# The low part of the prompt attention's values made by VectorE instead of GpSimd

## The chip, the cores and the metric

The kernel runs on one core of one Trainium2 chip. That core has five engines, each with a queue of its own that is worked in order: TensorE (PE in the profile, its weight loads PEld) multiplies matrices, VectorE (DVE) and ScalarE (ACT) work on whole tiles, GpSimd (POOL) does too and also issues some DMAs, SyncE (SP) issues the others. Tiles live in the on-chip memories, SBUF and, for TensorE's results, PSUM. The metric is the time of one execution on the device in microseconds (us), as the median of several runs; a profiled execution gives a trace beside it.

## The reference

One layer of a hybrid encoder is applied to a prompt of 2048 frames and, with the same weights, to 128 new frames (8 streams of 16) that attend to 1024 cached ones. Each layer is a normalization, one wide input projection, two branches, and an output projection:

```
h = rms_norm(x, norm_g);  z = h @ w_in
u_a, v_a, g_a, q, k, v, g_b = split(z)
y_a = u_a * spatial_gate(v_a) * silu(g_a)            # 4 groups, 128-position chunks
s = q.k / 8 - slope_h * |q_pos - k_pos|, masked by 64-position chunks, both halves c = 0, 1
a = softmax(s[0]) - lam * softmax(s[1])              # differential attention, 4 heads
o = rms_norm(a @ v) * const;  y_b = o * silu(g_b)
y = x + concat(y_a, y_b) @ w_out
```

The results are y for prompt and sample, and the new keys, values and gate rows. All of it is in 32-bit floating point.

## The kernel before

To keep precision, TensorE works on pairs: a value is split into a high part, which is the value rounded to the format fp32r, and a low part, the value less its high part. `mm3` (L491) then makes a product of three: high by high, high by low, low by high; in the profile every matmul stands under the line of a helper, L416, and every transpose under L420. `split` (L479 to L485) makes the two parts of a tile: ScalarE copies the source to the high part (L481), and then another engine subtracts (L482). That engine is VectorE unless the caller names one in the argument `lo_eng`.

The work has these stages, by the time in the profile:

- 0 to 830 us: `stream` runs the projections of the prompt and the sample (acc in the profile: 8 products of w and xT for each tile, head and kind), and beside them, woven in by `weave`, first the whole sample attention (`sample_attention`, names sk, sv, sa, sS, sO), then from 548 us on the prompt attention of the first half of the queries (`attention_a`).
- 830 to 940 us: the rest of the projections, and the output weights wo are loaded and split (tile wo, alternately by POOL and DVE).
- 940 to 1380 us: the prompt attention of the second half of the queries, beside the output products (`out_stream`, oo in the profile, with y_tp for the transposes of y and yT for their split).

The prompt attention (`attention`) goes head by head, and in a head by pairs of query tiles. `score_steps` makes the scores S in chunks of 512 keys; VectorE adds the distance term and takes the minimum (L911), ScalarE the exponential (L915), and the two halves are combined, by VectorE (L927) or by ScalarE and POOL (L930, L931). `value_steps` transposes the result (a_tp), splits it (aT) and multiplies it with the values v (oT).

The values come from `v_chunk` (L848 to L854). For each head and each 512 keys it loads vraw by a DMA on SP's queue (L851), into few buffers, and splits it into v, high and low (L853). There are 2 such chunks for each of 4 heads in the first half, and 3 and 4 for each head in the two groups of the second half: 8 + 12 + 16 = 36. The call in `v_chunk` names POOL for the subtraction. The buffers of v come free when the products oT of an earlier chunk are done; the buffer of vraw comes free when the subtraction has read it.

The order on each engine is not the order of the program's text. At the end, class `Order` takes all instructions, works out an estimated cost for each (`cost`, from its engine, kind and size), a due time, and dependences, and places them by simulating the engines (`run`); the order that it finds is fixed by added dependences. It also models that an operation of VectorE with two large inputs in SBUF and an operation of POOL shouldn't run at the same time (`port`). A changed engine of an instruction therefore changes the estimate, and with it possibly the place of every instruction after it, on every engine.

Of the kernel before, what the change touches and what calls it, by code (L numbers as in the profile page):

```python
# [55 lines left out]
def f(ap):  # L56
    return ap.bitcast(F32)
# [343 lines left out]
def trunk_step_kernel(  # L401
# [7 lines left out]
    act, dve, pool, sp = nc.scalar, nc.vector, nc.gpsimd, nc.sync  # L409
# [69 lines left out]
    def split(src, hi, lo, lo_eng=None, scale=None):  # L479
        if scale is None:  # L480
            act.copy(hi, src)  # L481
            (lo_eng or dve).tensor_tensor(out=lo, in0=src, in1=f(hi), op=ALU.subtract)  # L482
        else:
            act.activation(hi, src, AF.Copy, scale=scale)
            dve.scalar_tensor_tensor(out=lo, in0=src, scalar=scale, in1=f(hi), op0=ALU.mult, op1=ALU.subtract)  # L485
# [37 lines left out]
    def rows(ap):  # L523
        return ap.rearrange("(n p) e -> p n e", p=P)
# [323 lines left out]
    def v_chunk(sb, nv, h, g):  # L848
        r = slice(g * 512, (g + 1) * 512)
        raw = sb.tile([P, 4, P], F32, name="vraw", tag="vraw", bufs=cur["nraw"])  # L850
        sp.dma_start(raw, rows(nvp[r, h]))  # L851
        v = sb.tile([P, 2, 4, P], F32R, name="v", tag="v", bufs=nv)
        split(raw, v[:, 0], v[:, 1], pool)  # L853
        return v  # L854

    def q_load(sb, h, j, eng=sp):
# [133 lines left out]
    def attention(sb, sl, groups, wmax, nk, nv, nex, comb, eng):  # L990
# [12 lines left out]
        def v_step(key, c):  # L1003
            vs.setdefault(key, []).append(v_chunk(sl, nv, key[1], c))
            return 0
# [229 lines left out]
    with ExitStack() as left, ExitStack() as right:  # L1235
# [41 lines left out]
        for kc in range(8):  # L1277
            raw = p1.tile([P, D], F32, name="woraw", tag="x", bufs=2)
# [129 lines left out]
```

## Time and profile before

| what | us |
|---|---|
| median of 3 runs | 1381.08 (1380.9 to 1382.62) |
| profiled execution | 1381.83 |
| its span in the trace | 1380.1 |

The span is from the first to the last instruction of the trace. A busy time is the sum of an engine's instructions; "waited for" is the idle time of an engine just before an instruction and what released it. Matmuls overlap in TensorE's pipeline, and their ends are modelled, so a busy TensorE isn't yet one at its peak. The chain of waits follows the work that ended last back from the last instruction, at each step to what released it. Names such as v<-vraw say which tile is written and which are read; L482 is a line of the kernel, here that of the helper `split`, so that its callers are told apart by their tiles.

### The profile page before, as it was taken

How to read it: one execution, taken by the hardware profiler on the slowest of the kernel's cores; microseconds unless marked ns; L12 is line 12 of the kernel's file. 1: busy time of each engine (PE TensorE's matmuls, PEld its weight loads, DVE VectorE, ACT ScalarE, POOL GpSimd, SP SyncE). 2: the span in 40 equal slices, each digit the busy share in tenths (PEclk: the TensorE clock that was granted, in tenths of full speed). 3: DMA queues.
4: the chain of work that ended last, by engine and by line, in shares of the span. 5: the costliest groups of instructions: out<-in, count | busy, mean ns of one | idle time of the engine just before them, and what ended most of it. 6: DMA issues, size and time to landing. Idle time of an engine off the chain costs nothing.

```text
span 1380.1 us, 27913 instructions
## 1 busy us (share of the span) xinstructions
PE 1347.1 (98%) x9892; PEld 1260.5 (91%) x9892; DVE 925.7 (67%) x2286; ACT 791.2 (57%) x1778; POOL 452.1 (33%) x624
## 2 busy tenths in 40 slices
PE   5999999999999999999999999999999999999998
PEld 5999999999998999899999999998788888888887
DVE  4532338878777796678889775433889897887721
ACT  4433337766565785556676654223777776776620
POOL 2151530101010121656442323021565555454400
PEclk9999999999999999999999999999999999999999
DMA  6533334554445576635453325226646543442223
GB/s 213 178 83 102 83 76 130 174 153 135 142 124 151 157 226 187 173 93 157 108 148 100 98 66 157 77 73 214 187 144 180 140 133 107 145 131 81 84 89 104
DMA packets 209244, 183.05 MB, mean 133 GB/s; under 512 B 21104, under 2 KB 167024, under 8 KB 209104
## 3 DMA queue, kind: packets, MB, share of 16 engines
q1 hardware_dynamic: 199280, 155.17, 38.1%
q0 software_dynamic: 9824, 26.09, 7.0%
q8 instruction: 78, 1.28, 0.4%
q14 instruction: 62, 0.51, 0.1%
HBM read 130.86 MB, written 42.47 MB: 126 GB/s over the span
## 4 chain that ended last, share of the span: by engine, by line
PE 89%; DMA 4%; ACT 3%; DVE 2%; issue 1%; SPq 1%; POOL 0%; ACTq 0%; DVEq 0%
PE acc L416 44%; PE oo L416 13%; PE S L416 9%; PE oT L416 7%; PE a_tp L420 4%; PE sS L416 2%; PE sk_tp L420 2%; PE sO L416 2%; PE y_tp L420 1%; DMA svraw<-in_cache_v_dram 1%; PE mix L416 1%; PE x_tp L420 1%; DMA wraw<-in_w_in_dram 1%; PE k_tp L420 1%; ACT sa L1142 1%
## 5 line engine op out<-in xcount | busy, mean ns | idle before, releaser
L416 PE MATMUL acc<-w,xT 128*128 128x256 f32 x5376 | 715.3, 283 | 3.6 <-DVE w L649 1.8
L416 PEld LDWEIGHTS acc<-w,xT 128*128 128x128 f32 x5376 | 675.6, 190 | 13.8 <-DVE w L649 2.3
L416 PE MATMUL oo<-wo,yT 128*128 128x512 f32 x816 | 231.7, 400 | 1.3 <-ACT yT L481 1.3
L416 PE MATMUL S<-kT,qT 128*128 128x512 f32 (+3 forms) x688 | 186.5, 361 | 2.2 <-DVE sst L911 2.1
L915 ACT ACTIVATE ex<-ex,sst 128x128 f32<-128x128 f32 (+15 forms) x128 | 153.9, 1203 | 41.1 <-DVE sst L911 40.2
L416 PEld LDWEIGHTS oo<-wo,yT 128*128 128x128 f32 x816 | 146.5, 188 | 26.6 <-ACT yT L481 1.8
L416 PE MATMUL oT<-aT,v 128*128 128x256 f32 x864 | 150.7, 293 | 0.2 <-ACT aT L481 0.2
L649 DVE SCALAR_TENSOR_TENSOR w<-wraw,normg,w 128x256 fp32r<-128x256 f32 x224 | 105.5, 496 | 57.9 <-ACT w L648 56.5
L911 DVE CUSTOM_DVE_ANT_0 ex<-S,dist,sst 128x512 f32<-128x512 f32 (+2 forms) x192 | 123.6, 652 | 29.0 <-PE S L416 27.8
L648 ACT ACTIVATE w<-wraw,normg 128x256 fp32r<-128x256 f32 x220 | 104.4, 505 | 57.3 <-DMA wraw<-in_w_in_dram 40.3
L416 PEld LDWEIGHTS S<-kT,qT 128*128 128x128 f32 x688 | 112.6, 189 | 18.1 <-DVE sst L911 6.1
L416 PEld LDWEIGHTS oT<-aT,v 128*128 128x128 f32 x864 | 120.8, 189 | 4.5 <-ACT aT L481 0.5
L481 ACT CAST aT<-a_tp 128x512 fp32r<-128x512 f32 (+1 forms) x144 | 79.7, 561 | 65.3 <-PE a_tp L420 63.3
L482 DVE TENSOR_TENSOR aT<-a_tp,aT 128x512 fp32r<-128x512 f32 (+1 forms) x144 | 93.6, 658 | 27.6 <-ACT aT L481 25.7
L911 DVE CUSTOM_DVE_ANT_0 ex<-S,dist 128x512 f32<-128x512 f32 (+3 forms) x128 | 79.2, 629 | 21.4 <-PE S L416 16.5
L488 POOL TENSOR_SCALAR vst<-vst 128x2 f32<-128x2 f32 (+1 forms) x36 | 9.0, 250 | 257.3 <-ACT vn L743 256.4
L420 PE MATMUL a_tp<-ident,ex 128*128 128x128 f32 x544 | 88.6, 274 | 1.3 <-DVE ex L927 0.9
L420 PEld LDWEIGHTS a_tp<-ident,ex 128*128 128x128 f32 x544 | 64.7, 140 | 13.1 <-DVE aT L482 2.5
L931 POOL TENSOR_TENSOR ex<-ex 128x1024 f32<-128x1024 f32 (+4 forms) x32 | 58.7, 1849 | 23.8 <-ACT ex L930 23.7
L482 DVE TENSOR_TENSOR sv<-svraw,sv 128x512 fp32r<-128x512 f32 (+1 forms) x72 | 50.3, 700 | 22.4 <-ACT sv L481 21.6
L481 ACT CAST sv<-svraw 128x512 fp32r<-128x512 f32 (+1 forms) x72 | 44.3, 618 | 32.6 <-DMA svraw<-in_cache_v_dram 15.0
L927 DVE SCALAR_TENSOR_TENSOR ex<-ex,sst 128x1024 f32<-128x1024 f32 (+4 forms) x64 | 62.1, 970 | 0.9
(144 smaller groups left out, 1901.1 us busy)
## 6 DMA issues: line engine op xcount, KB each, us to landing
wraw<-in_w_in_dram SPq DMA_DIRECT2D x160, 128.0 KB, 2.9
skraw<-in_cache_k_dram SPq DMA_DIRECT2D x64, 256.0 KB, 2.9
svraw<-in_cache_v_dram SPq DMA_DIRECT2D x64, 256.0 KB, 3.0
kT<-k_scr POOLq DMA_DIRECT2D x20, 512.0 KB, 5.2
vraw<-out_dram SPq DMA_DIRECT2D x36, 256.0 KB, 3.1
y<-y_scr SPq DMA_DIRECT2D x34, 256.0 KB, 2.9
out_dram<-xo SPq DMA_DIRECT2D x34, 256.0 KB, 2.2
wraw<-in_w_in_dram SPq DMA_DIRECT2D x128, 64.0 KB, 2.4
```

The costliest lines, as they stand in the source:

```text
L416: pe.last = nc.tensor.matmul(*a, **k).ins
L420: pe.last = nc.tensor.transpose(*a, **k).ins
L481: act.copy(hi, src)
L482: (lo_eng or dve).tensor_tensor(out=lo, in0=src, in1=f(hi), op=ALU.subtract)
L488: pool.tensor_scalar(out=ms, in0=ms, scalar1=1.0, scalar2=EPS, op0=ALU.mult, op1=ALU.add)
L648: act.activation(w[:, 0], r, AF.Copy, scale=normg[:, kc:kc + 1])
L649: dve.scalar_tensor_tensor(out=w[:, 1], in0=r, scalar=normg[:, kc:kc + 1], in1=f(w[:, 0]), op0=ALU.mult, op1=ALU.subtract)
L911: dve.tensor_tensor_reduce(out=ex[c][:, a:b], in0=s, in1=dist[:, off + a:off + b], scale=SLOPES[h], scalar=prev[c], op0=ALU.add, op1=ALU.m ...
L915: act.activation(ex[c][:, :w], ex[c][:, :w], AF.Exp, bias=prev[c], scale=-1.0, accum_out=st[:, c, 6:7])
L927: dve.scalar_tensor_tensor(out=p0, in0=p1, scalar=st[:, 1, 7:8], in1=p0, op0=ALU.mult, op1=ALU.add)
L931: pool.tensor_tensor(out=p0, in0=p1, in1=p0, op=ALU.add)
L1142: act.activation(a[r:r + 32], p[c1], AF.Copy, scale=st[c1, 6:7])
```

## The change

In `v_chunk` the last argument of `split` is dropped, so that VectorE makes the low part of v. Nothing else is edited; the planner works out a new order with it.

```
@@ -850,7 +850,7 @@
         raw = sb.tile([P, 4, P], F32, name="vraw", tag="vraw", bufs=cur["nraw"])
         sp.dma_start(raw, rows(nvp[r, h]))
         v = sb.tile([P, 2, 4, P], F32R, name="v", tag="v", bufs=nv)
-        split(raw, v[:, 0], v[:, 1], pool)
+        split(raw, v[:, 0], v[:, 1])
         return v
```

More of the change, by code (lines that the diff above doesn't have):

```diff
@@ L852, in v_chunk @@
         v = sb.tile([P, 2, 4, P], F32R, name="v", tag="v", bufs=nv)
-        split(raw, v[:, 0], v[:, 1], pool)
+        split(raw, v[:, 0], v[:, 1])
         return v
```

## The prediction

> **What bounds the kernel now.** I read the page first, then the busy time by stage, then the chain of waits, then who ended TensorE's waits.
>
> ```profile
> span 1380.1 us, 27913 instructions
> PE 1347.1 (98%) x9892; PEld 1260.5 (91%) x9892; DVE 925.7 (67%) x2286; ACT 791.2 (57%) x1778; POOL 452.1 (33%) x624
> PE 89%; DMA 4%; ACT 3%; DVE 2%; issue 1%; SPq 1%; POOL 0%; ACTq 0%; DVEq 0%
> ```
>
> TensorE (PE) is busy for 98% of the span, and 89% of the chain that ended last is its own work; POOL has 0% of it and VectorE (DVE) 2%. So an edit that only moves work between POOL and DVE has little to win or lose directly; it acts only where PE comes to wait. The stages come next: from 548 us on the prompt attention runs, at first beside the projections, from 940 us beside the output product. Each row has the stretch, its length, then busy time (and instructions) of PE, PEld, DVE, ACT and POOL.
>
> ```profile
> 548.00:600.00 52.00, 48.82 (x397) 47.39 (x396) 32.67 (x76) 29.42 (x74) 35.40 (x43) 1.00 0.57 152
> 600.00:700.00 100.00, 100.00 (x810) 97.86 (x809) 85.35 (x216) 63.85 (x161) 52.22 (x76) 1.00 0.45 123
> 700.00:830.00 130.00, 128.54 (x1027) 124.87 (x1026) 103.95 (x279) 82.37 (x239) 42.92 (x88) 1.00 0.37 100
> 940.00:1000.00 60.00, 56.96 (x309) 46.17 (x308) 39.98 (x105) 35.63 (x64) 27.09 (x32) 1.00 0.59 180
> 1000.00:1100.00 100.00, 99.67 (x626) 87.05 (x625) 86.60 (x222) 77.53 (x151) 59.15 (x76) 1.00 0.54 154
> 1100.00:1200.00 100.00, 100.00 (x610) 86.79 (x609) 81.82 (x207) 70.07 (x118) 51.74 (x62) 1.00 0.45 128
> 1200.00:1300.00 100.00, 100.00 (x620) 87.64 (x619) 80.92 (x202) 67.92 (x117) 46.37 (x51) 1.00 0.35 103
> 1300.00:1380.00 80.00, 76.07 (x389) 62.66 (x388) 22.19 (x36) 17.44 (x35) 9.03 (x12) 1.00 0.28 96
> ```
>
> DVE is the second engine in every one of these stages up to 1300 us, and fullest at 1000 to 1100 us: 86.60 of 100 us, 13.4 us free. POOL is never over 60% there except in the 52 us after 548 (35.40, 68%). In the chain of waits of 1000 to 1300 us, this is the line of shares, and the one long piece that is not PE's:
>
> ```profile
> by line: PE oo L416 33.1%; PE S L416 26.7%; PE oT L416 20.5%; PE a_tp L420 12.4%; PE y_tp L420 2.7%; PE o_tp L420 0.9%; PE q_tp L420 0.9%; PE k_tp L420 0.9%; DVE ex L927 0.7%; DVE ex L911 0.6%; issue 0.2%; DVE aT L482 0.2%; DVE qT L485 0.1%
> 1045.27 1.98 DVE ex L927
> ```
>
> The PE shares add up to 98.1%. Last, who ended PE's waits: the four longest rows of 540 to 830 us, one of 830 to 940, four of 940 to 1300 (total us, times, longest). Every row left out is 0.3 us or less.
>
> ```profile
> PE acc L416 <- DVE w L649: 1.8, 1, 1.8
> PE S L416 <- DVE sst L911: 1.6, 2, 1.4
> PE q_tp L420 <- DMA qraw<-q_scr: 1.2, 1, 1.2
> PE sO L416 <- ACT sv L481: 0.9, 1, 0.9
> ...
> PE oo L416 <- ACT yT L481: 1.0, 1, 1.0
> ...
> PE q_tp L420 <- DMA qraw<-q_scr: 1.3, 1, 1.3
> PE a_tp L420 <- DVE ex L927: 0.9, 2, 0.6
> PE S L416 <- DVE sst L911: 0.5, 2, 0.2
> PE a_tp L420 <- DVE aT L482: 0.3, 1, 0.3
> ```
>
> They sum to 9.5 us. That is all that a better order of the other engines could win from 540 us on, and no row names v: PE has never waited for these values.
>
> **The change, part by part.** Removed are 36 subtractions on POOL, added the same 36 on DVE, with the same operands: vraw and the high part, both in SBUF, 128x512 f32. The rows of groups by shape have the POOL one, and a DVE one of exactly this form, the sample's values. The third row, of the tile wo, has min/median/max in ns for the same form on DVE in a stretch where POOL splits the other half of wo.
>
> ```profile
> L482 POOL TENSOR_TENSOR v<-vraw,v 128x512 fp32r<-128x512 f32 x36 | 47.3, 1315 | 37.7 <-ACT v L481 36.0 <-DVE sst L911 1.4
> L482 DVE TENSOR_TENSOR sv<-svraw,sv 128x512 fp32r<-128x512 f32 x64 | 43.9, 687 | 21.7 <-ACT sv L481 20.9
> L482 DVE TENSOR_TENSOR wo<-woraw,wo x8: 678/684/1605, 828.4 to 856.6; 128x512 fp32r<-128x512 f32 x8
> ```
>
> POOL loses 47.3 us. DVE gains 36 x 0.687 = 24.7 us. At its worst one costs 1.605 us, the wo that I take to have stood behind a POOL operation; I take 0.687, since seven of eight there are near 0.684 and the planner keeps DVE operations with two SBUF inputs and POOL ones apart where it can. The moved instruction also brings a wait: on DVE, in order, it stands before whatever is queued behind it until ScalarE's high part is there. The nearest price is the same pair in the sample stage: 20.9 us over 64, 0.33 us each. Behind it on DVE stand the score minima (L911), the low parts of aT and the sums L927, for which PE's S, oT and a_tp wait. So one costs DVE between 0.69 and 1.02 us. Where they fall, from the stages of the tile v (PE, PEld, ACT, POOL busy):
>
> ```profile
> 548.00:600.00 52.00, 1.03 (x6) 0.85 (x6) 1.21 (x2) 3.02 (x2) 1.00 0.57 152
> 940.00:1000.00 60.00, 7.20 (x42) 5.85 (x42) 3.08 (x5) 6.71 (x5) 1.00 0.59 180
> 1000.00:1100.00 100.00, 32.12 (x186) 26.18 (x186) 5.56 (x9) 11.73 (x9) 1.00 0.54 154
> 1100.00:1200.00 100.00, 28.78 (x168) 23.10 (x168) 4.38 (x7) 9.05 (x7) 1.00 0.45 128
> 1200.00:1300.00 100.00, 31.27 (x180) 25.20 (x180) 4.35 (x7) 9.06 (x7) 1.00 0.35 103
> ```
>
> *Steady stages, 1000 to 1300 us: 23.* In the fullest, 9 x 0.687 = 6.2 us brings DVE from 86.6 to 92.8 of 100 us, with the wait for ScalarE to 95.8. It still fits, and what hides it is PE's own queue: while S waits, PE has the output product, 33% of the chain. I count nothing here. If that cover is gone, the price is up to 6.2 us in this stage (below, as a rival). One thing goes: the L927 at 1045.27 took 1.98 us, where its form has a mean of 1.31,
>
> ```profile
> L927 DVE SCALAR_TENSOR_TENSOR ex<-ex,sst 128x1024 f32<-128x1024 f32 x24 | 31.4, 1310 | 0.3
> ```
>
> while a POOL subtraction of v was running, and PE's a_tp waited behind it: of the two waits of 0.9 us in all it is the shorter one, 0.3 us. I take 0.3 us off; ends 0 and 0.3 off.
>
> [...]
>
> *Start of the second attention, 940 to 1000 us: five.* Here DVE is in the chain. Of the pieces around the third of the five, and of the place near 564 us where the second v of the first attention falls:
>
> ```profile
> 564.49 0.69 DVE qst L684
> 565.20 1.08 DVE qT L876
> ...
> 976.84 0.69 DVE aT L482
> 977.53 0.39 DVE ex L911
> ```
>
> At 977 us DVE works without a gap on the chain and a v is due: I count the full 0.7 us for this one; for the other four nothing, since DVE is busy for only 39.98 of these 60 us and stands idle shortly after each. Ends: 0 and 1.4 (two of them).
>
> *548 to 600 us: two.* The first falls into idle time; the second competes with the chain at 564 us. I take 0.3 us (less than one subtraction, since a gap follows soon); ends 0 and 0.7.
>
> *600 to 830 us: the six that are left of the 36.* PE is full and DVE has 14.65 us (100 - 85.35) and 26 us (130 - 103.95) free; the six are 4.1 us. One is on the chain:
>
> ```profile
> 760.96 1.31 POOL v L482
> 762.28 0.37 SPq L851
> 763.10 4.97 DMA qraw<-q_scr
> ```
>
> SP's next vraw waits until this subtraction has read the buffer, and behind it on SP stands the load of qraw, for which PE waits 1.2 us. On DVE the subtraction is 0.62 us shorter (1.31 - 0.69), but may start later. I take 0.2 us off; ends 0.6 off and 0.7 more.
>
> *830 to 940 and after 1300 us: none.* At the end the cover is large: after the last scores (before 1300 us) DVE is busy for 22 of 80 us, and PE has long runs of its own, such as
>
> ```profile
> 1307.33 10.69 PE oo L416 x47
> ```
>
> so an attention that ends a few microseconds later only lets this run come earlier. POOL's DMA issues (L824, L844, L878, L879) move up in its queue; nothing on the chain waits for them.
>
> The sum: 0.3 - 0.2 + 0.7 - 0.3 = +0.5 us; with all ends, from -0.9 to +2.8. The profiled execution took 1381.83 us for its span of 1380.1; by it the time would be 1382.3. The median of the runs is 1381.08, so I forecast 1381.6. About 0.2%, 2.8 us, is what a measurement of this kernel can tell from no change; the whole sum lies within it.
>
> **The rivals.** *DVE becomes the bound (slower).* The place is 1000 to 1100 us: if the 13.4 us that DVE has free there are not free when the 9 subtractions come, because each has to come soon after ScalarE's part and before the scores behind it, then S waits for its minima and PE for S, and the output product can't fill since its own low parts (yT L482) stand in the same queue. The price is 6.2 us for this stage: 1381.6 + 6.2 = 1387.8; if it took all 23 of 1000 to 1300 us, 15.8 us. It decides from the point at which PE waits for DVE in this stage for more than about 2.3 us. For it: DVE is fuller here than anywhere. Against it: PE's waits for DVE in 940 to 1300 us now sum to 1.7 us with DVE at 80 to 87%. [...] I give it 0.24.
>
> *The freed POOL and the new order take waits away (faster).* The planner orders every engine by its own estimate of costs, POOL's subtractions and the port they hold included; with 47.3 us of POOL gone, L927, the POOL sums and SP's vraw come earlier, and about half of the 9.5 us of PE's waits goes: 1381.1 - 4.8 = 1376.3. For it: the waits for qraw and L927 hang behind a POOL subtraction in part. Against it: those behind DVE (w, sst) get no shorter by a fuller DVE. I give it 0.16.
>
> That the change doesn't do what it says I rule out: one argument falls to its default, DVE.
>
> **How the numbers follow.** No change within 2.8 us: 0.60, its own range 1379.9 to 1383.9. Slower 0.24, faster 0.16. From 1376.5 to 1387.5 the range leaves out about half of the slower rival's chance and half of the faster one's, 0.20 in all.
>
> **What would show it.** In the profile after: 36 DVE rows of v near 0.69 us and none on POOL; DVE near 950 us, POOL near 405; DVE at 1000 to 1100 us near 93; the span's PE busy time unchanged; the wait for qraw near 767 us smaller. The forecast is wrong if PE's waits for DVE from 940 us on grow by over 2.8 us (the first rival), or if the sum of PE's waits falls by as much (the second). A v among the names that PE waits for would be a mechanism that I have not priced.

## The result, and the profile after

| | before | after |
|---|---|---|
| median of 4 runs each, us | 1380.99 (1377.54 to 1382.62) | 1389.49 (1389.14 to 1392.34) |
| profiled execution, us | 1381.83 | 1389.14 |
| its span, us | 1380.1 | 1387.4 |

The change makes the kernel slower: after to before is 1.0066, 95% interval 1.0048 to 1.0083, some 8.5 us. The forecast was 1381.6, and its range ended at 1387.5.

The head of the page of after: span, busy times, shares of the chain that ended last.

```profile
span 1387.4 us, 27900 instructions
PE 1350.0 (97%) x9892; PEld 1262.1 (91%) x9892; DVE 949.8 (68%) x2322; ACT 791.2 (57%) x1778; POOL 408.1 (29%) x588
PE 84%; DVE 4%; DMA 4%; ACT 4%; issue 2%; SPq 1%; POOL 0%; DVEq 0%; ACTq 0%; POOLq 0%
```

DVE and POOL came out as forecast (near 950 and 405). But PE's share of the chain fell from 89% to 84%. The windows by stage of after, columns as before:

```profile
940.00:1000.00 60.00, 55.91 (x295) 46.31 (x294) 41.95 (x108) 33.59 (x60) 20.42 (x27) 0.97 0.57 168
1000.00:1100.00 100.00, 99.26 (x623) 85.45 (x622) 89.19 (x232) 77.10 (x147) 47.08 (x66) 1.00 0.52 152
1100.00:1200.00 100.00, 96.03 (x581) 83.19 (x580) 86.53 (x206) 67.49 (x118) 39.47 (x52) 0.98 0.43 122
1200.00:1300.00 100.00, 99.38 (x609) 86.50 (x608) 86.24 (x211) 69.02 (x116) 39.06 (x46) 1.00 0.38 111
```

The stage that loses is not the one where DVE is fullest. At 1000 to 1100 us, with DVE at 89.19, PE is still busy for 99.26; at 1100 to 1200 us, with DVE at 86.53, PE drops from 100.00 to 96.03, and the granted clock, 1.00 before in every stage, reads 0.98. It reads 0.97 at 940 to 1000 us. Who ended PE's waits from 940 to 1300 us in after:

```profile
PE oT L416 <- DVE aT L482: 4.6, 3, 3.4
PE q_tp L420 <- DVE qT L485: 1.8, 1, 1.8
PE a_tp L420 <- DVE ex L927: 1.0, 1, 1.0
PE S L416 <- DVE sst L911: 0.6, 1, 0.6
PE a_tp L420 <- DVE aT L482: 0.5, 1, 0.5
PE y_tp L420 <- DVE qT L485: 0.4, 1, 0.4
```

One wait of 3.4 us stands out. Its row names aT, not v: the name is that of the last instruction before PE could go on, and what held that one up must be looked for in DVE's queue. The groups by shape and the tile's own row (min/median/max in ns) have it:

```profile
L482 DVE TENSOR_TENSOR v<-vraw,v 128x512 fp32r<-128x512 f32 x36 | 31.5, 875 | 1.6 <-ACT v L481 1.1 <-DMA gbt<-g_scr 0.4
```

```profile
L482 DVE TENSOR_TENSOR v<-vraw,v x36: 669/684/4494, 556.3 to 1292.8; 128x512 fp32r<-128x512 f32 x36
```

The median is the forecast's 0.684, the mean is 0.875, and one of the 36 took 4.494 us. Here it is, in the timelines of DVE, POOL and PE of after (start, duration; in brackets the idle time before, and who ended it):

```profile
1140.86 0.69 DVE L482 TENSOR_TENSOR aT<-a_tp,aT 128x512 fp32r<-128x512 f32 x1 [0.83 <-ACT aT L481]
1141.47 4.49 DVE L482 TENSOR_TENSOR v<-vraw,v 128x512 fp32r<-128x512 f32 x1
1145.89 0.74 DVE L911 CUSTOM_DVE_ANT_0 ex<-S,dist,sst 128x512 f32<-128x512 f32 x1
...
1146.56 0.68 DVE L482 TENSOR_TENSOR aT<-a_tp,aT 128x512 fp32r<-128x512 f32 x1
```

```profile
1141.82 2.12 POOL L931 TENSOR_TENSOR ex<-ex 128x896 f32<-128x896 f32 x1
1143.87 0.32 POOL L961 MEMSET aT<- 128x256 f32 x1
1144.14 1.26 POOL L1332 TENSOR_TENSOR xo<-yo,xo 128x512 f32<-128x512 f32 x1
```

```profile
1143.54 0.39 PE L416 MATMUL oo<-wo,yT 128*128 128x512 f32 x1
1147.29 0.86 PE L416 MATMUL oT<-aT,v 128*128 128x256 f32 x5 [3.36 <-DVE aT L482]
```

v starts, and 0.35 us later POOL's sum L931 does. v ends at 1145.96, 0.56 us after the last of three POOL operations (1144.14 + 1.26 = 1145.40). The median of the 36 is 0.684 us, so by these times it made next to no progress until POOL was through with all three. Behind it on DVE stand L911 and the aT that PE's next matmul needs, and none of the output products that come after oT on PE ran ahead of it: PE, with work left, stands still for 3.36 us. Two more subtractions, at 1176.31 and 1278.08 us, took 1.81 and 2.08 us beside a POOL L931 (started at 1176.00 and 1278.05 us), and PE waited 0.6 us for each.

Where the time went is seen, in these two profiled executions, by setting each matmul's start against that of the same matmul before (the k-th of the same tile names). After less before is +1.3 us at 433 us, ahead of the first v and so no effect of it; -2.1 at 938; +0.9 at 985; +1.0 at 1119; +7.3 at the end. The first attention thus gained 3.4 us, the start of the second lost 3.0, and from 1119 us on 6.3 are lost.

### The profile page after: what moved, and what is told of

Read it like the earlier page. It is cut to its first block, busy times and chain, and to the rows that moved or that the text cites. A ratio compares the mean times of both kernels' runs of the same rounds, so it can differ in the third digit from the quotient of the medians.

```text
span 1387.4 us, 27900 instructions
## 1 busy us (share of the span) xinstructions
PE 1350.0 (97%) x9892; PEld 1262.1 (91%) x9892; DVE 949.8 (68%) x2322; ACT 791.2 (57%) x1778; POOL 408.1 (29%) x588
## 4 chain that ended last, share of the span: by engine, by line
PE 84%; DVE 4%; DMA 4%; ACT 4%; issue 2%; SPq 1%; POOL 0%; DVEq 0%; ACTq 0%; POOLq 0%
PE acc L416 43%; PE oo L416 12%; PE S L416 8%; PE oT L416 6%; PE a_tp L420 4%; PE sS L416 2%; PE sO L416 2%; PE sk_tp L420 2%; DMA x<-in_x_prompt_dram 1%; PE y_tp L420 1%; DVE ex L911 1%; DMA wraw<-in_w_in_dram 1%; DVE aT L482 1%; PE x_tp L420 1%; PE mix L416 1%
## 5 line engine op out<-in xcount | busy, mean ns | idle before, releaser
L915 ACT ACTIVATE ex<-ex,sst 128x512 f32<-128x512 f32 (+15 forms) x128 | 153.9, 1203 | 41.0 <-DVE sst L911 40.4
L416 PE MATMUL oT<-aT,v 128*128 128x256 f32 x864 | 153.5, 296 | 4.6 <-DVE aT L482 4.6
L911 DVE CUSTOM_DVE_ANT_0 ex<-S,dist,sst 128x512 f32<-128x512 f32 (+2 forms) x192 | 123.2, 651 | 25.6 <-PE S L416 24.0
L911 DVE CUSTOM_DVE_ANT_0 ex<-S,dist 128x512 f32<-128x512 f32 (+3 forms) x128 | 78.9, 630 | 21.5 <-PE S L416 17.1
L931 POOL TENSOR_TENSOR ex<-ex 128x1024 f32<-128x1024 f32 (+4 forms) x32 | 59.4, 1863 | 51.0 <-ACT ex L930 50.8
L927 DVE SCALAR_TENSOR_TENSOR ex<-ex,sst 128x1024 f32<-128x1024 f32 (+4 forms) x64 | 61.0, 953 | 0.8
```

What stands on the lines that cost most here:

```text
L416: pe.last = nc.tensor.matmul(*a, **k).ins
L911: dve.tensor_tensor_reduce(out=ex[c][:, a:b], in0=s, in1=dist[:, off + a:off + b], scale=SLOPES[h], scalar=prev[c], op0=ALU.add, op1=ALU.m ...
L915: act.activation(ex[c][:, :w], ex[c][:, :w], AF.Exp, bias=prev[c], scale=-1.0, accum_out=st[:, c, 6:7])
L927: dve.scalar_tensor_tensor(out=p0, in0=p1, scalar=st[:, 1, 7:8], in1=p0, op0=ALU.mult, op1=ALU.add)
L931: pool.tensor_tensor(out=p0, in0=p1, in1=p0, op=ALU.add)
```

## The experiments

Three theories stood against each other. **Port** (after the planner's `port`): v's subtraction is shut out while POOL's operations run, as it seems at 1141 us, and PE's stop costs clock beside. **Load:** DVE is too full, the prediction's slower rival. **Order:** the planner's new order is worse by itself. A ratio below is the time over that of the kernel before, with its 95% interval. The kernels were timed beside the kernel before on the same chip, whose medians were 1379.91 (25 runs), 1381.01 (25 runs) and 1381.0 us (29 runs).

**The collision taken away.** Same kernel and same order on every engine as after; but a POOL operation of over 1 us that is planned next after a v on DVE waits for it. First for all, then (second kernel) only for the one v near 1141 us. In the code `at` holds the planned starts.

```
+ at = {}
  ...
+ at[i] = t
  ...
+ sync = mybir.DependencyInfo(mybir.DependencyClass.Sync, mybir.DependencyReason.DATA)
+ for n in N:
+     if n.engine == self.DVE and n.writes and n.writes[0].bass_ap.tensor.name.startswith("v_"):
+         b = next((b for b in out[self.POOL] if at[b] >= at[n.idx] and port[b] and self.cost(N[b])[0] > 1000), None)
+         if b is not None:
+             self.tc.add_manual_dep(N[b].ins, n.ins.name, sync, reason="port")
```

> The changed kernel, same order on every engine; the one addition is that the POOL operation of over 1 us that the planner put next after a v subtraction waits for that subtraction. Port theory (the subtraction at 1141 us was shut out by two POOL operations for 3.8 us, TensorE stood idle for 3.4 us and then ran at about half its clock for 4 us; two more were shut out for 1.1 and 1.4 us): no v row over 1.3 us after 940 us, the 3.4 us wait and the clock's dip near 1150 us gone, so 5 to 7 us off, about 1383 us. Load theory (DVE is simply too full with 25 us more): no change, 1389 us. Order theory (the new order is by chance worse in many small places): no change, 1389 us.

Measured: 1380.46 us (1378.73 to 1384.4), ratio 1.0007 (0.9997 to 1.0017), some 2.5 us below the expected 1383. The tile's row, the same place in POOL's timeline, and the stages of 1000 to 1300 us, of the kernel with all fences:

```profile
L482 DVE TENSOR_TENSOR v<-vraw,v x36: 671/682/1210, 553.6 to 1284.3; 128x512 fp32r<-128x512 f32 x36
```

```profile
1140.43 2.12 POOL L931 TENSOR_TENSOR ex<-ex 128x896 f32<-128x896 f32 x1 [0.46 <-DVE v L482]
```

```profile
1000.00:1100.00 100.00, 99.28 (x616) 85.16 (x615) 89.48 (x230) 77.15 (x147) 49.42 (x67) 1.00 0.53 154
1100.00:1200.00 100.00, 100.00 (x610) 86.72 (x610) 86.21 (x216) 70.86 (x121) 42.45 (x55) 1.00 0.44 130
1200.00:1300.00 100.00, 100.00 (x621) 87.47 (x620) 84.13 (x207) 68.02 (x117) 39.35 (x45) 1.00 0.33 99
```

DVE carries the same load (89.48, 86.21, 84.13 against 89.19, 86.53, 86.24), the order is the same, and PE is full. So neither load nor order makes the 8.5 us. Between these two traces the order of the matmuls is the same, so each step can be read off: after loses 5.0 us at 1141 and 0.9 each at 1176 and 1278 us; from 1119 us to the end it is 6.7 in all (the steps are rounded).

> The changed kernel in its own order with one single added wait: only the POOL operation after the subtraction near 1141 us waits for it (the other 35 have none). Port theory, now borne out for all together: this one place is worth the 3.4 us of idle TensorE and about 1.8 us of its slow clock, and what else the shut-out delayed; the rows of 1.8 and 2.1 us near 1176 and 1278 us may come back and cost up to 0.7 us each. So 1381 to 1384 us, and at least 5 us below the change. If the loss were spread over many short waits: 1387 us or more.

Measured with one fence: 1382.6 us (1380.17 to 1383.96), ratio 1.0011 (1.0001 to 1.002). The two short collisions stay (0.9 us each again), and the tile's row and PE's waits from 1100 to 1300 us show them:

```profile
L482 DVE TENSOR_TENSOR v<-vraw,v x36: 671/684/2065, 554.3 to 1283.8; 128x512 fp32r<-128x512 f32 x36
```

```profile
PE oT L416 <- DVE aT L482: 1.2, 2, 0.6
```

One dependence, at one of 36 places, takes back most of the loss: the ratio to before falls from 1.0066 to 1.0011.

**Each half of the change alone.** Only the 8 chunks of the first attention on DVE, then only the 28 of the second.

```
- split(raw, v[:, 0], v[:, 1])
+ split(raw, v[:, 0], v[:, 1], dve if nv == 2 else pool)    # the other kernel: pool if nv == 2 else dve
```

> Only the 8 subtractions of the first attention move to DVE; the 28 of the second stay on POOL. Port theory: the loss lay in the second attention, and the first one gained about 3 us, so 1377 to 1380 us. Load theory: 8 of 36 of the loss, about 1383 us. Order theory: anything from 1377 to 1389, by the new order.

> Only the 28 subtractions of the second attention move to DVE. Port theory: slower than the change, 1388 to 1393 us, if v rows over 1.3 us come in it again, and near 1381 us if none does. Load theory: 28 of 36 of the loss, about 1388 us, with or without long v rows. Order theory: anything from 1377 to 1393.

Measured: 1379.12 us (1376.59 to 1382.47), ratio 0.9994 (0.9983 to 1.0004), for the first; 1389.29 (1387.53 to 1392.58), 1.0071 (1.0053 to 1.0089), for the second. The second half holds the whole loss. Its order up to 940 us is another than that of after, and yet the same v (at 1140.69 us) meets the same POOL operations for the same time:

```profile
L482 DVE TENSOR_TENSOR v<-vraw,v x28: 672/684/4496, 943.0 to 1291.1; 128x512 fp32r<-128x512 f32 x28
```

**The order alone.** The kernel before, POOL and all, with the planner's estimate of POOL's subtraction of v raised by 30 ns, then by 90 ns: enough for another order on every engine from the first v on.

```
- t = 190 + 2.16 * size if kind == "TensorTensor" else 195 + 1.1 * size
+ t = (190 + 30 * n.writes[0].bass_ap.tensor.name.startswith("v_")) + 2.16 * size if kind == "TensorTensor" else 195 + 1.1 * size
```

> The kernel before, v on POOL as it was; only the planner's estimate of that subtraction is 30 ns longer, which gives another order from the first of them on. It measures what another order is worth by itself. Order theory: the time moves by several us, up to 8. Port and load theory: within 3 us of before, 1378 to 1384 us, unless a DVE operation with two SBUF inputs is shut out for long somewhere.

> Second measure of what another order is worth by itself: the kernel before, v on POOL, the planner's estimate of that subtraction 90 ns longer. As the first one gave the same time as before, 1378 to 1383 us; over 1385 us would say that orders alone can cost as much as the change did.

Measured: 1379.04 us (1377.94 to 1383.64), ratio 0.9997 (0.9986 to 1.0008), and 1380.95 (1378.26 to 1382.31), 1.0001 (0.9991 to 1.001). Two new orders by themselves moved the median by less than 1 us. In the first of them the stretch from 521 to 843 us got 3.1 us shorter too, with no v on DVE: such a gain in the first attention needs no more than another order than before's (in the second kernel it is 1.0).

**The wait without POOL.** To see what a late v costs when POOL has no part in it, the fully fenced kernel gets one useless DVE operation right ahead of the v near 1141 us, in three sizes (3x512 below, then 5 and 7 for the 3). The planner is told that it costs nothing (those lines are left out below), so no order changes.

```
+ split(raw, v[:, 0], v[:, 1]); cnt.append(0); len(cnt) == 25 and dve.reduce_sum(ctile([P, 8], "dly")[:, :3], fl(f(v[:, 0])).unsqueeze(1).broadcast_to([P, 3, 512]), axis=AX.X)
```

> The fenced kernel (every subtraction protected from POOL) in the same order; VectorE gets one useless sum of 3x512 elements, about 1.7 us, just before the subtraction near 1141 us. It needs one SBUF input and no POOL. If the delay alone matters and not the port as such, TensorE is idle there for about 1.3 us. Clock theory (a long idle time of TensorE is followed by some us at half clock, a short one is not): no dip of the clock near 1150 us, about 1.3 us more than the fenced kernel, 1382 us. Delay-only theory: the same here.

> The same with a sum of 7x512 elements, about 3.9 us, the length of the shut-out in the changed kernel. Clock theory: TensorE idle for about 3.4 us, then a granted clock near 0.5 to 0.6 for some 4 us, so about 5 us more than the fenced kernel, 1385 to 1386 us. Delay-only theory: no dip, 3.4 us more, 1384 us. If the loss of the change needed the port lock itself and not a delay: no loss here.

> As the 3x512 and 7x512 delays, with 5x512: one useless VectorE operation of about 2.8 us stands before the v near 1141 us. Interpolated, TensorE idles 2.2 to 2.3 us before oT. If the clock loses only after an idle stretch of nearly 3.3 us, the cost at this place is about 2.7 us over the fence alone (1.6 at 3x512 plus 1.1), 1382.5 to 1383.5 us and no window under 0.9; if the loss sets in at any idle over about 2 us, it is 5 us and more, 1385 to 1386 us, with windows near 0.5.

| delay on DVE | PE idle before oT | shift of the matmuls from 1155 to 1300 us, against the fenced kernel | median, ratio |
|---|---|---|---|
| 3x512, 1.74 us | 1.17 us | +1.7 us | 1381.72, 1.0006 (0.9997 to 1.0015) |
| 5x512, 2.81 us | 2.26 us | +3.7 us | 1382.99, 1.0013 (1.0003 to 1.0023) |
| 7x512, 3.88 us | 3.35 us | +6.0 us | 1386.32, 1.0044 (1.0029 to 1.0059) |

With the same stop of PE as in after, 3.35 us, and no collision, 6.0 us are lost, where after loses 5.0: a stop of this length costs by itself, and the collision with POOL is only what made it. The idle time is a part; the rest is the clock. Windows of 0.5 us, the clock third from the end of the line, of after and then of the 7x512 delay:

```profile
1148.00:1148.50 0.50, 0.50 (x5) 0.41 (x4) 0.50 (x1) 0.50 (x1) 0.00 (x0) 0.92 1.73 306
1148.50:1149.00 0.50, 0.50 (x3) 0.40 (x2) 0.47 (x3) 0.48 (x2) 0.00 (x0) 0.50 0.28 57
...
1151.00:1151.50 0.50, 0.50 (x5) 0.50 (x4) 0.00 (x0) 0.50 (x1) 0.00 (x0) 0.50 0.05 16
1151.50:1152.00 0.50, 0.50 (x5) 0.50 (x5) 0.00 (x0) 0.50 (x1) 0.00 (x0) 0.67 0.00 0
```

```profile
1145.00:1145.50 0.50, 0.00 (x0) 0.00 (x0) 0.50 (x2) 0.00 (x0) 0.27 (x1) 0.73 0.00 0
...
1152.00:1152.50 0.50, 0.50 (x6) 0.50 (x6) 0.00 (x0) 0.50 (x3) 0.00 (x0) 0.94 0.93 344
```

In after the clock is half for a time: it reads 0.50 in every window from 1148.50 to 1151.50 us, 0.92 is then 0.08 us of that window at half, 0.67 is 0.33, so from 1148.42 to 1151.83 us, 3.41 us, of which I count half, 1.7, as lost. With the idle 3.36 that is 5.1, and 5.0 was measured. With the 7x512 delay it is half from 1145.23 to 1152.06 us, 6.83 us; 5.65 of these lie after PE started again at 1146.41 and cost 2.8, with the idle time 6.2 for 6.0 measured. The 5x512 delay, worked out in the same way, has 3.41 us from 1144.56 on, 3.2 of them after PE's start at 1144.79: with the idle 2.26 that is 3.9 for 3.7 measured. Its expectation had the clock lost either not at all or for over 5 us in sum; neither held: the clock was halved for one such stretch, and the sum is 3.7. (The 1.7 us of the 3x512 delay are 0.5 more than its idle time, at a clock of 1.00 in each stage from 1000 to 1300 us; that is not explained.)

**No low part at all.** This kernel leaves the low part of v out and takes the high part in its place in the second product, so PE's work stays.

```
- split(raw, v[:, 0], v[:, 1])
+ act.copy(v[:, 0], raw)                       # and in oT: v[:, 0] where v[:, 1] was
```

> v's low part is left out altogether (the product that used it takes the high part, so TensorE's work stays and the result is less exact). It shows what the 36 subtractions cost the kernel before on whatever engine. If they only cost where they collide (Port), the time is that of the fenced kernel with the freed places, 1377 to 1380 us; if VectorE's or POOL's load counts (Load), several us less, under 1375.

Measured: 1380.76 us (1379.37 to 1384.28), ratio 1.0003 (0.9993 to 1.0014). To have none of the 36 subtractions on any engine wins nothing that can be told from none (expected were 1377 to 1380 by the port theory, under 1375 by the load theory). So there was nothing to win by moving them.

**A version meant to beat both.** The fenced kernel, with the five v at 940 to 1000 us on POOL.

```
- split(raw, v[:, 0], v[:, 1])
+ cnt.append(0); split(raw, v[:, 0], v[:, 1], pool if 9 <= len(cnt) <= 13 else dve)
```

> VectorE makes v's low part in 31 of 36 chunks, POOL in the five that fall at the start of the second attention (9th to 13th), and a POOL operation over 1 us that is planned next after a v on VectorE waits for it. Port theory with its second place: the first attention keeps its gain (offset near -4 us at 938 us), the start of the second attention loses no more than 0.5 us there instead of the 3.2 of the fence alone, nothing is lost from 1000 us on: 1377 to 1378.5 us, that is 1 to 3 us under the kernel before; PE's wait q_tp <- DVE qT near 967 us is gone. If the loss at 960 to 974 us is not from v on VectorE but from the order, it stays: 1380 to 1381 us.

Measured: 1379.62 us (1376.3 to 1383.39), ratio 0.9992 (0.9981 to 1.0004): above what was expected, and no gain that can be told from none. The mechanism fits in part: against before it loses 0.6 us from 938 to 985 us, where the kernel with all fences loses 2.9, and DVE's qT is gone from PE's waits there. But a wait for a DMA has come in its place, and the clock still falls to half from 969.94 us on for 3.4 us:

```profile
PE q_tp L420 <- DMA qraw<-q_scr: 1.7, 1, 1.7
```

## Why the prediction was wrong, point by point

**The step that failed** is the one on the steady stages, 1000 to 1300 us: "what hides it is PE's own queue ... I count nothing here", with each operation at 0.687 us because "the planner keeps DVE operations with two SBUF inputs and POOL ones apart where it can". Both halves failed at the same places. The planner keeps them apart in its own timetable alone, and fixes only the order within each engine, not between two. In that timetable this L931 begins just where v ends; in the run the aT ahead of v had to wait for ScalarE (0.83 us of idle time on DVE), POOL had no such wait, and they met. The 1.605 us of wo, which I took for one collision, was my worst price of one operation; behind three POOL operations in a row the same form took 4.49. And PE's cover, 33% output products, was of no use there: PE's next instruction was oT, and nothing behind it ran in the 3.36 us. Measured against the fenced kernel, this term is 6.7 us instead of -0.3, and the fence takes it away.

Which of the two starts first did not tell which one was held up. At 1141 us v starts 0.35 us ahead of L931, at 1176 and 1278 us 0.31 and 0.03 us behind it, and v is the one that waits each time (4.49, 1.81 and 2.08 us for a median of 0.684), while the L931 at 1141 us takes 2.12 us, as with the fence. Nor did v get in during the 0.20 us between L931 and L1332 (1143.94 to 1144.14), in which POOL has only the memset. No run separates whether the memset held it off, or this gap is too short.

**Start of the second attention, 940 to 1000 us: +0.7 forecast, +3.0 measured.** The v that matters is not the one I picked at 977 us but one at 961.31. From DVE's timeline of after, ScalarE's, PE's, and PE's clock:

```profile
961.31 0.67 DVE L482 TENSOR_TENSOR v<-vraw,v 128x512 fp32r<-128x512 f32 x1
961.89 0.74 DVE L911 CUSTOM_DVE_ANT_0 ex<-S,dist,sst 128x512 f32<-128x512 f32 x1
...
962.57 0.27 DVE L920 TENSOR_SCALAR sst<-sst,neglam 128x1 f32<-128x1 f32 x1
```

```profile
962.93 1.15 ACT L930 ACTIVATE ex<-ex,sst 128x1024 f32<-128x1024 f32 x1 [1.31 <-DVE sst L920]
```

```profile
968.10 0.41 PE L420 MATMUL q_tp<-ident,qraw 128*128 128x128 f32 x2 [1.79 <-DVE qT L485]
969.51 1.06 PE L420 MATMUL a_tp<-ident,ex 128*128 128x128 f32 x8 [0.99 <-DVE ex L927]
```

```profile
970.00:972.00 2.00, 1.78 (x13) 1.58 (x12) 1.56 (x3) 1.51 (x4) 1.68 (x3) 0.73 0.79 261
972.00:974.00 2.00, 2.00 (x11) 2.00 (x10) 1.84 (x4) 0.45 (x2) 0.81 (x2) 0.50 0.93 190
974.00:976.00 2.00, 2.00 (x17) 1.93 (x17) 1.39 (x2) 1.69 (x3) 0.00 (x0) 0.91 1.17 307
```

Here v is at its normal 0.67 us. It stands on DVE ahead of L911 and L920, ScalarE waits 1.31 us for L920 and is later with everything behind it, qT (L484) among it, for which DVE and then PE wait. That this is v's doing and not the order's is argued from this chain. The traces agree: from 938 to 1119 us the seven kernels with these five on DVE lose 2.8 to 4.7 us against before, and the five others with them on POOL or left out 0.0 to 0.6; but the order differs too.

From 960 to 978 us PE stands idle for 3.0 us, and for 2.5 before, and the clock, 1.00 before, goes to half for 3.41 us, up to 1.7 us more. This half clock is not v's mark. The clock of 940 to 1000 us reads 0.97 in the kernel without any low part and in the one with the first half alone as well, and 1.00 in the kernel with one fence, whose matmuls stand in the same order as those of after:

```profile
940.00:1000.00 60.00, 55.29 (x306) 45.59 (x305) 44.58 (x115) 37.20 (x65) 21.24 (x28) 1.00 0.52 148
```

That kernel still loses 2.3 us from 938 to 985 us, with PE idle for 3.6 us from 960 to 978. So the greater part of the loss at this place needs no half clock.

**548 to 830 us: +0.1 forecast, -3.4 measured.** This is the faster rival's effect, at its place, and for a part of its price: PE's waits for w (1.8), sst (1.6) and sv (0.9) are gone, and those of over 0.3 us are a DMA of qT (1.0), qT (0.8) and qraw (0.4); v is named now too, at 0.3, a mechanism that I had not priced. The order-only kernel's 3.1 us from 521 to 843 us, as many as after's, show that VectorE isn't needed for it. One execution doesn't fix its size: kernels with the order of after gain 2.8 to 4.9 us in this stretch. That it nearly makes up for the loss at 940 to 1000 us is luck. With only this half of the change the median is still within 0.2% of before.

**The slower rival** named the right side and nearly the time (1387.8), by the wrong mechanism. Its mark was PE waiting for DVE for over 2.3 us at 1000 to 1100 us; it was 0.7 there (aT 0.5, yT 0.2), and with the same load and the fence the time is that of before. Its larger sign, waits for DVE from 940 us on grown by over 2.8 us, did appear (from 1.7 to 9.1), which shows that such a sign doesn't tell a full engine from a blocked one.

**Right:** the median price of 0.684, the load on DVE and POOL, the L927 of 1.98 us gone (the longest is 1.329 now), no cost from 600 to 830 us or after 1300 us, the wait for qraw that shrank (1.2 to 0.4 us), and that the moved work cost nothing measurable on POOL; with the fence it costs nothing measurable on DVE either (ratio 1.0007).

## What to carry to other kernels

An operation is not priced by its median alone: the v of after have a median of 0.684 us, and one of the 36 took 4.494 beside POOL's operations. Look at what the other engine runs around each place that it moves to, add up the other's operations in a row, and ask what stands behind it on its own queue. A planner's "not at the same time" holds only if a dependence between the two engines says so; one such dependence was worth some 5 us here by the traces. And a stop of TensorE of 2.26 us (5x512 delay) or 3.36 us (after) had a second price here, 3.4 us at half clock, while behind one of 1.17 us (3x512 delay) the clock stayed at 1.00.

## What the runs showed of the hardware

**A blocked VectorE operation wasn't let in between POOL operations that followed each other.** At 1141 us it stayed out through L931, a memset and L1332, 4.494 us in after and 4.496 in the kernel with the second half alone, for a normal 0.684.

**The granted clock fell for 3.41 us, or for twice that.** From 400 to 1375 us after has two such losses, 3.41 us from 1148.42 us on and, by the same reckoning from the 2 us windows above, from about 970.9 to 974.3 us. With the 5x512 delay the clock is half for 3.41 us from 1144.56 us on, with the 7x512 delay for 6.83 from 1145.23 us on. The two of after begin 177.5 us apart, which is 52 times 3.41 within the rounding. The start keeps no fixed distance from the stop: 0.2 us before PE goes on with the 5x512 delay, 1.1 us behind it in after. So I divide the time before each loss into stretches of the same 3.41 us. The one just before had PE idle for 2.3 us (after, 1145.01 to 1148.42), 2.0 (5x512), 2.2 (7x512), and 1.8 in three pieces (after, 967.5 to 970.9). A stretch at half with 1.2 us idle was followed by a second one at half (7x512, 1145.23 to 1148.64); one at half with PE busy throughout was followed by a clock of 1.00 (after, 1148.42 to 1151.83; 7x512, 1148.64 to 1152.06).

The idle time alone does not decide. After 1.7 us idle (after, 428.21 to 431.62) the clock stayed at 1.00, and in the kernel before it did so with 2.3 us idle in the 3.41 us from 426.20 to 429.61 us. After 1.1 us idle it fell with the 3x512 delay:

```profile
987.31:990.72 3.41, 2.33 (x12) 1.24 (x10) 2.24 (x10) 3.39 (x6) 3.36 (x3) 1.00 0.40 119
990.72:994.14 3.42, 3.39 (x9) 2.76 (x10) 3.34 (x7) 0.61 (x2) 1.19 (x3) 0.50 0.69 153
```

The stage from 940 to 1000 us reads 0.94 in all three delay kernels, where after has 0.97. What counts beside the idle time stays open.
